# Stick-breaking attention in one hybrid decoder step: Q and K first, then prompt heads and sample pages in one schedule

## The chip, the core and the metric

The kernel runs on one core of one Trainium2 chip. The metric is the device time of one execution in microseconds (us). A core has these engines: PE (TensorE, matrix products and transposes; PEld is its weight load), DVE (VectorE), ACT (ScalarE), POOL (GpSimd) and SP (SyncE, which here issues the DMA transfers). Each executes its own instructions in order and waits on semaphores for the others.

## What is computed

One inference step of a decoder with two layers and model width 1024. Layer 0 mixes tokens by a causal convolution, layer 1 by stick-breaking attention (16 heads of 64); a SwiGLU FFN follows each. There are 512 prompt tokens, and a sample group of 8 sequences with 8 new tokens each, whose 1024 past keys and values lie in a paged pool (8 pages of 128 rows for each sequence, found through a page table). All 576 tokens share the weights. The attention, cut to what matters:

```python
def sb_attend(q, k, v, q_pos, bias):
    z = einsum('bthd,bshd->bhts', q, k) * HEAD_DIM ** -0.5 + bias
    causal = arange(tk) < q_pos
    log_1m_beta = where(causal, -softplus(z), 0.0)
    after = cumsum(log_1m_beta, reverse=True) - log_1m_beta
    a = where(causal, exp(log_sigmoid(z) + after), 0.0)
    return einsum('bhts,bshd->bthd', a, v)
# prompt: q, k, v of the 512 tokens, in blocks of 128 queries
# sample: k and v are the pages of the pool, then the 8 new rows
```

The rows of K and V of all new tokens are outputs too. Everything is fp32.

## The kernel before

Features lie on partitions and tokens in columns (576, as two halves of 288). An fp32 product with weights is made of three products of rounded parts: a tile is split into a high part (`hi`, a cast on ACT) and a low part (`lo`, a subtraction on DVE), and hi·hi, lo·hi and hi·lo are summed. The weights stream in as 512 KB chunks (`wraw`) and are split into `whi` and `wlo`; the activations' parts are `ahi` and `alo`. The attention layer comes in this order:

- The V product (L1372) for all heads. ACT brings each bank to a buffer `vf` (L1378), from which the V rows are stored and the parts `bhi`, `blo` are split.
- Q and K products, 16 chunks of 128 features (`gemm_piece`, L1403), and between them the prompt heads, two per chunk pair `t`. A head's Q and K are split into stacks `qst`, `kst` that hold hi and lo on 128 partitions (L1425 to L1439), so that `z` is two products (L1472) and a causal mask added by a third (L1473). For each block of 128 queries: two sigmoids on ACT, 1-beta (`om`) and beta (`be`) (L1482); the running product of `om`, a scan on DVE (L1492); the weight, a product on POOL (L1499); transposes of the weight on PE (`at`, L1506); the split of the transposed weight into `athi` and `atlo` (L1512 to L1516); and eight products with V (`prompt_o`, L1524). K rows for the output are transposed on PE, copied to the buffer `ktok` (L1457) and stored from SP.
- The order of this stage comes from a list schedule (`graph`, `run_ops`): each operation has an engine, a planned cost and the resources that it reads and writes, and the program emits the operations in planned order. Each engine then keeps that order. A few tables (`LAG`, `Q_AT`, `K_AT`, `K0_AT`, `AT_DVE`) say at which block the next chunk's product goes in and which engine splits.
- The sample's pages: 32 groups (8 sequences, four pairs of pages each), in an order written out by hand (`step(n)`). Each group loads two K pages (`kr`) and two V pages (`vr`) of 512 KB; transposes K on PE (`kt`, L1608, 16 of them), copied to `kts` by ACT and DVE (L1613); makes `sz` for all heads in four blocks of 32 rows (L1628); two sigmoids (L1645, L1651), a scan (L1667) that carries on from the group before, a multiply (L1676); two transposes of the weights (`sat`, L1691) with their copy (L1693); and products with V in four blocks of 32 columns (`so`, L1707).
- The output projection `wo` for the first halves of three of its eight chunks runs at the end of the pages. `ffn(1, ..., 3, ...)` does the rest of it together with the second FFN.

Of the kernel before, what the change touches and what calls it, by code (L numbers as in the profile page):

```python
# [9 lines left out]
F32 = mybir.dt.float32  # L10
# [6 lines left out]
P = 128  # L17
D = 1024
# [23 lines left out]
AT_DVE = (((0, 0, 1, 0), (1, 1, 0, 1)), ((0, 0, 0, 1), (0, 1, 1, 0)), ((1, 0, 1, 1), (0, 0, 1, 0)), ((1, 0, 1, 1), (0, 0, 1, 0)), ((1, 1, 1, 0), (1, 1, 1, 0)), ((0, 1, 1, 0), (0, 0, 0, 1)), ((1, 1, 1, 1), (0, 1, 1, 0)), ((1, 0, 1, 0), (0, 0, 0, 1)))  # L42
LAG = 1
Q_AT = 0
K_AT = 2
K0_AT = (0, 5, 6, 7)
NVR = 8
# [14 lines left out]
def hybrid_step_kernel(  # L62
# [11 lines left out]
    base = ctx.enter_context(tc.tile_pool(name="base", bufs=1))  # L74
# [212 lines left out]
    x = base.tile([P, NT, TOK], F32, name="x")  # L287
    ahi = base.tile([P, NT, TOK], F32R, name="ahi")
    alo = base.tile([P, NT, TOK], F32R, name="alo")
    bhi = base.tile([P, NT, TOK], F32R, name="bhi")  # L290
    blo = base.tile([P, NT, TOK], F32R, name="blo")
    sacc = base.tile([P, TOK], F32, name="sacc")
    rbc = base.tile([P, TOK], F32, name="rbc")
    rtok = base.tile([P, 8], F32, name="rtok")
# [1051 lines left out]
    with tc.tile_pool(name="att", bufs=1) as att:  # L1346
        qkn = [att.tile([P, NT, TS], F32, name=f"{c}n") for c in "qk"]
# [3 lines left out]
        kts = [att.tile([P, NT, GW], F32, name="kts0")]  # L1351
# [5 lines left out]
        with cvps, tc.tile_pool(name="pr", bufs=1) as pp:  # L1357

            for half in range(2):
                cs = slice(half * 512, (half + 1) * 512)  # L1360
                ps = [bank("mm", f"v{half}_{i}") for i in range(4)] + [bank("z", f"v{half}_4")]
                for kp in range(4):
                    whi, wlo, _ = w_next()
                    if half == 0 and kp == 2:
                        stat_a("mix1")
                    if half == 1 and kp == 2:
                        stat_b("mix1")
                    for k2 in range(2):
                        k = 2 * kp + k2
                        for j, (a, w) in enumerate(((ahi, whi), (ahi, wlo), (alo, whi))):  # L1370
                            for i, (c0, n) in enumerate(TT):
                                nc.tensor.matmul(  # L1372
                                    ps[i][0:n, :], a[:, k, c0 : c0 + n], w[:, k2, :],
                                    start=(k == 0 and j == 0), stop=(k == NT - 1 and j == 2),
                                )
                for i, (c0, n) in enumerate(TT):
# [12 lines left out]
            qst = pp.tile([P, 2, 2, TP], F32R, name="qst")  # L1389
            athi = pp.tile([P, 13, P], F32R, name="athi")  # L1390
            atlo = pp.tile([P, 13, P], F32R, name="atlo")
            base = state["got"]
            qfs, kparts, kfs, amat, pos = {}, {}, {}, {}, {}

            gps = {}

            def gemm_piece(t, which, k):
                if k == 0:
                    gps[t, which] = [bank("mm", f"{'qk'[which]}{t}_{i}") for i in range(2)]
                whi, wlo, nk = parts[base + 2 * t + which]  # L1400
                for j, (w, r) in enumerate(((whi, ahi), (whi, alo), (wlo, ahi))):
                    for i in range(2):
                        nc.tensor.matmul(  # L1403
                            gps[t, which][i][:, :HALF], w[:, k, :], r[:, k, HS[i]],
                            start=(k == 0 and j == 0), stop=(k == nk - 1 and j == 2),
                        )

            def gemm_out(t, which):
                parts.pop(base + 2 * t + which)
                f = pp.tile([P, TOK], F32, tag=f"f{which}", name=f"f{which}_{t}", bufs=2 - which)  # L1410
# [181 lines left out]
            def kt(n):  # L1592
                return kts[n % 2]
# [455 lines left out]
```

## Time and profile before

| What | Value |
|---|---|
| time, median of 3 runs | 1605.6 us (1604.29 to 1607.52) |
| the profiled execution, time | 1609.35 us |
| its span, first to last instruction | 1607.6 us |
| mean granted TensorE clock | 0.984 of full speed |
| PE busy | 1510.4 us (94%) |
| PEld busy | 1352.6 us (84%) |
| DVE busy | 1248.0 us (78%) |
| ACT busy | 782.3 us (49%) |
| POOL busy | 407.2 us (25%) |
| DMA, whole span | 180.23 MB, mean 112 GB/s |

A share over the whole span says little here, since the stages have different limits: about 24 of 40 equal slices of the span lie ahead of the pages and show 4 to 103 GB/s (184 in the first); the four slices of the pages show 293 to 407. So the profile is read by stages: a table of busy times by stretch, then single instructions in order of time, whose distances give prices. A busy PE is not PE at its peak, since entries of matmuls overlap in it; the distance from one start to the next is the better price.

### The profile page before, as it was taken

What the parts mean: (1) busy time and instruction counts of PE and PEld (TensorE: products, weight loads), DVE (VectorE), ACT (ScalarE), POOL (GpSimd) and SP (SyncE); (2) the same over time, 40 slices, a digit from 0 to 9 for tenths busy, and PEclk for the clock granted to TensorE, in tenths of its full rate; (3) what the DMA queues carried; (4) which work ended last, traced back from release to release, by engine and by line L of the source; (5) the groups of instructions that cost most, each with busy time, mean ns of one, the idle gap of its engine ahead of it and who ended that gap; (6) DMA issues with size and microseconds to landing.
All of it is one profiled execution on the core that took longest, in us unless ns stands there. A gap on an engine that the chain in (4) does not pass through costs nothing. (4 is left out here: it accounts for less than half of the span.)

```text
span 1607.6 us, 35925 instructions
## 1 busy us (share of the span) xinstructions
PE 1510.4 (94%) x14371; PEld 1352.6 (84%) x14371; DVE 1248.0 (78%) x2155; ACT 782.3 (49%) x1665; POOL 407.2 (25%) x410
## 2 busy tenths in 40 slices
PE   7999989899999999999999988999998999999997
PEld 7996559889999999987988875555797999999997
DVE  5998544699989999982689985555459998999884
ACT  5223123355546545552667664444435554654553
POOL 3110211333323322350244450000132322332210
PEclk9999998999999999999999989999999999999999
DMA  6233001023222233233321227999612222232231
GB/s 184 76 88 87 4 5 38 29 80 92 93 92 89 85 103 93 70 89 95 91 68 43 73 81 293 407 406 398 217 37 66 92 93 94 90 93 93 92 101 64
DMA packets 152047, 180.23 MB, mean 112 GB/s; under 512 B 6106, under 2 KB 130530, under 8 KB 151864
## 3 DMA queue, kind: packets, MB, share of 16 engines
q1 hardware_dynamic: 151448, 176.36, 33.2%
q8 instruction: 113, 1.85, 0.5%
q10 hardware_dynamic: 432, 1.57, 0.3%
q14 instruction: 54, 0.44, 0.1%
HBM read 170.45 MB, written 8.18 MB: 111 GB/s over the span
## 5 line engine op out<-in xcount | busy, mean ns | idle before, releaser
L953 DVE TENSOR_TENSOR wlo<-fs,whi 128x512 fp32r<-128x512 f32 (+1 forms) x256 | 233.5, 913 | 26.8 <-ACT whi L135 18.8
L1095 PE MATMUL fb<-ahi,whi 128*128 128x288 f32 x704 | 210.7, 299 | 14.2 <-ACT ft L135 9.4
L135 ACT CAST whi<-fs 128x512 fp32r<-128x512 f32 (+1 forms) x256 | 157.1, 614 | 134.9 <-PE fb L1095 115.6
L1095 PE MATMUL fb<-xe,whi 128*128 128x288 f32 x1056 | 216.1, 297 | 0.1
L1095 PE MATMUL fb<-alo,whi 128*128 128x288 f32 x704 | 207.7, 295 | 7.9 <-DVE alo L953 7.9
L1095 PE MATMUL fb<-ahi,wlo 128*128 128x288 f32 x704 | 211.1, 300 | 2.3 <-DVE wlo L953 2.3
L1095 PEld LDWEIGHTS fb<-xe,whi 128*128 128x128 f32 x1056 | 170.4, 189 | 0.5 <-issue 0.3
L1095 PE MATMUL fb<-xe,wlo 128*128 128x288 f32 x528 | 159.1, 301 | 2.7 <-DVE wlo L953 2.6
L1095 PEld LDWEIGHTS fb<-ahi,whi 128*128 128x128 f32 x704 | 133.3, 189 | 17.9 <-ACT ft L135 12.4
L1095 PEld LDWEIGHTS fb<-alo,whi 128*128 128x128 f32 x704 | 134.4, 191 | 8.8 <-DVE alo L953 8.8
L1095 PEld LDWEIGHTS fb<-ahi,wlo 128*128 128x128 f32 x704 | 133.2, 189 | 5.0 <-DVE wlo L953 5.0
L953 DVE TENSOR_TENSOR wlo<-wraw,whi 128x512 fp32r<-128x512 f32 (+1 forms) x160 | 124.0, 782 | 5.7 <-ACT whi L135 5.2
L135 ACT CAST whi<-wraw 128x512 fp32r<-128x512 f32 (+1 forms) x160 | 98.0, 613 | 51.8 <-PE fb L1095 46.0
L1095 PEld LDWEIGHTS fb<-xe,wlo 128*128 128x128 f32 x528 | 99.6, 189 | 7.5 <-DVE wlo L953 7.1
L135 POOL TENSOR_TENSOR fs<-wraw 128x512 f32<-128x512 f32 (+1 forms) x32 | 47.1, 1473 | 210.5 <-DVE wlo L953 210.5
L223 ACT CAST whi<-wraw 128x1024 fp32r<-128x1024 f32 (+1 forms) x43 | 44.9, 1044 | 110.7 <-PE cb L585 48.3
L135 POOL TENSOR_TENSOR fs<-wraw,fs 128x512 f32<-128x512 f32 (+1 forms) x64 | 86.0, 1343 | 50.5 <-DVE wlo L953 44.2
L135 POOL TENSOR_TENSOR fs<-fr 128x512 f32<-128x512 f32 (+1 forms) x32 | 43.7, 1364 | 208.3 <-DVE wlo L953 208.3
L1095 PE MATMUL fb<-he,whi 128*128 128x288 f32 x456 | 93.0, 297 | 2.1 <-DVE x L135 2.0
L628 PE MATMUL cb<-up,dg 32*32 32x288 f32 (+1 forms) x3584 | 80.6, 385 | 13.8 <-issue 13.5
L1095 PE MATMUL fb<-bhi,whi 128*128 128x288 f32 x304 | 90.3, 297 | 2.1 <-DVE x L135 2.1
L1095 PE MATMUL fb<-bhi,wlo 128*128 128x288 f32 x304 | 90.1, 296 | 0.0
(375 smaller groups left out, 4078.1 us busy)
## 6 DMA issues: line engine op xcount, KB each, us to landing
kr<-in_cache_k_dram SPq DMA_DIRECT2D x64, 512.0 KB
vr<-in_cache_v_dram SPq DMA_DIRECT2D x64, 512.0 KB
wraw<-in_ffn_w_up_dram SPq DMA_DIRECT2D x44, 512.0 KB
wraw<-in_cv_w_pw_dram SPq DMA_DIRECT2D x24, 512.0 KB
wraw<-in_ffn_w_down_dram SPq DMA_DIRECT2D x24, 512.0 KB
wraw<-in_sb_w_qkv_dram SPq DMA_DIRECT2D x23, 512.0 KB
fr<-in_ffn_w_gate_dram SPq DMA_DIRECT2D x22, 512.0 KB
wraw<-in_ffn_w_gate_dram SPq DMA_DIRECT2D x22, 512.0 KB
```

Source lines behind the costliest of these rows:

```text
L135: ops[i][3](*(a() if callable(a) else a for a in ops[i][4]))
L223: nc.scalar.copy(hi[:, :n], raw[:, :n])
L628: nc.tensor.matmul(banks[bs[i]][rj, 0:n], dgs[d][ri, k, :], ups[t][ri, h * HALF + k : h * HALF + k + n], start=(m == 0), stop=(k >= PET - ...
L953: nc.vector.tensor_sub(dst, a, b.bitcast(F32))
L1095: nc.tensor.matmul(banks[b][:, :HALF], w[:, k, :], r[:, k, :], start=(first and k == 0 and j == 0), stop=(k == nk - 1 and j == 2), skip_gr ...
```

## The change

- V is no longer split. ACT writes it in fp32 to `vt`, which takes the place of `bhi`, and it is stored from there. `blo` becomes room for the transposed weights `at` and the scan outputs `prd`.
- Q and K are kept in fp32 for all tokens (`qf`, `kf`); the 16 chunks of their products come first, with only the transposes of K rows between them. These go out through a tag `sq` of two buffers, which later holds the prompt's `be`.
- Then one list schedule holds eight head pairs and 32 page groups. The pair `t` is emitted ahead of group `3t`. `z` of a pair is two fp32 products of 64 rows each at row positions 0 and 64 (L1439), `prompt_o` fp32 products of 64 columns at column positions 0 and 64 (L1478), so each head of a pair has half of the array's rows, or of its columns. The stacks, the split of the weights and the sum of two output parts go away; the outputs replace Q in `qf` and are split once at the end.
- V pages lie in `ahi` and `alo` (eight places), K pages in `whi` and `wlo` (two groups deep).
- `wo` has two first halves ahead of the FFN; `ffn(1, ..., 2, ...)` does one half more.

The diff, cut to its core:

```diff
-LAG = 1
-Q_AT = 0
-K_AT = 2
-K0_AT = (0, 5, 6, 7)
-NVR = 8
...
+    with cvps, tc.tile_pool(name="att", bufs=1) as att:
+        vflat = flat_of(renew("bhi", "vt", F32))
+        vt = vflat[:, 0 : 4 * D].rearrange("p (i c) -> p i c", c=D)
+        oflat = flat_of(renew("blo", "at", F32))
+        at_ = [oflat[:, e * 13 * P : (e + 1) * 13 * P].rearrange("p (r q) -> p r q", q=P) for e in range(2)]
+        prd = [oflat[:, 26 * P + i * (TP + 4) : 26 * P + i * (TP + 4) + TP + 1] for i in range(2)]
+        qk = [att.tile([P, NT, TOK], F32, name=f"{c}f") for c in "qk"]
+        kts = [att.tile([P, NT, GW], F32, name=f"kts{i}") for i in range(2)]
...
-                    vf = pp.tile([P, 512], F32, tag="vf", name=f"vf{half}_{i}", bufs=2)
-                    nc.scalar.activation(vf[0:n, :], ps[i][0:n, :], AF.Copy, scale=rtok[0:n, i : i + 1])
-                    if i < 4:
-                        hs = slice(4 * half, 4 * half + 4)
-                        vv = vf.rearrange("p (t e c) -> p t e c", e=2, c=DH)
-                        split_to(bhi[:, hs, c0 : c0 + DH], bhi[:, hs, c0 + DH : c0 + P], vv[:, :, 0, :])
-                        split_to(blo[:, hs, c0 + DH : c0 + P], blo[:, hs, c0 : c0 + DH], vv[:, :, 1, :])
-                        nc.sync.dma_start(v_prompt[c0 : c0 + n, cs], vf)
-                    else:
-                        nc.vector.tensor_copy(vn[:, cs], vf[0:n, :])
-                        nc.sync.dma_start(v_sample[:, cs], vf[0:n, :])
...
+            for i, (c0, n) in enumerate(TT):
+                dst = vt[:, i, cs] if i < 4 else vn[:, cs]
+                nc.scalar.activation(dst, ps[i][0:n, :], AF.Copy, scale=rtok[0:n, i : i + 1])
+                nc.sync.dma_start(v_prompt[c0 : c0 + n, cs] if i < 4 else v_sample[:, cs], dst)
...
+        def k_out_put(t, part, b):
+            fs = slice(t * P, (t + 1) * P)
+            ktok = small.tile([P, TOK], F32, tag="sq", name=f"ktok{t}_{part}", bufs=2)
+            if part == 0:
+                nc.scalar.copy(ktok[:, 0:TP], banks[b])
+                nc.sync.dma_start(
+                    k_prompt.rearrange("(i p) f -> p i f", p=P)[:, :, fs],
+                    ktok[:, 0:TP].rearrange("p (i c) -> p i c", c=P),
...
-                for j in range(2):
-                    nc.tensor.matmul(pzt[:, 0:n], qst[:, e, j, qs], kst[:, e, 0:n], start=(j == 0), stop=False)
-                nc.tensor.matmul(pzt[:, qb * P : n], identb, mask, start=False, stop=True)
+        def z_pe(t, qb):
+            n = (qb + 1) * P
+            qs = slice(qb * P, n)
+            for e in range(2):
                 hs = slice(e * DH, (e + 1) * DH)
+                nc.tensor.matmul(
+                    banks[e][:, 0:n], qk[0][hs, t, qs], qk[1][hs, t, 0:n], start=True, stop=False,
+                    tile_position=(e * DH, 0),
                 )
+            for e in range(2):
+                nc.tensor.matmul(banks[e][:, qb * P : n], identb, mask, start=False, stop=True)
...
+        def at_put(e, qb, b, eng):
+            dst = at_[e][:, slice(qb, qb + 3 * qb + 1, 3), :]
+            src = banks[b][:, 0 : (qb + 1) * P].rearrange("p (j q) -> p j q", q=P)
+            (nc.vector.tensor_copy if eng == "D" else nc.scalar.copy)(dst, src)
...
-                for j in range(4):
-                    r = slice(4 * j, 3 * j + 4)
-                    for i, b in enumerate((athi, atlo)):
-                        nc.tensor.matmul(
-                            po[:, j * P : TP], (bhi, blo)[e][:, t, j * P : (j + 1) * P], b[:, r, :],
-                            start=(j == 0 and i == 0), stop=(j == 3 and i == 1),
+        def prompt_o(t, b):
+            for j in range(4):
...
+                    nc.tensor.matmul(
+                        banks[b][hs, j * P : TP], vt[:, j, (2 * t + e) * DH : (2 * t + e + 1) * DH], at_[e][:, r, :],
+                        start=(j == 0), stop=(j == 3), tile_position=(0, e * DH),
+                    )
...
+        def prompt_put(t, b):
+            nc.vector.tensor_copy(qk[0][:, t, 0:TP], banks[b])
...
+                kr = wpool.tile([P, D], F32R, tag=("whi", "wlo")[i], name=f"kr{c}").bitcast(F32)
+                gather(kr, cache_k, c)
+                kraw[n].append(kr)
...
+        def open_v():
+            for tag in ("ahi", "alo"):
+                a = flat_of(renew(tag, f"v_{tag}", F32))
+                vplace.extend(a[:, i * D : (i + 1) * D] for i in range(4))
+                satp.append(a[:, 4 * D : 4 * D + 3 * P].rearrange("p (i c) -> p i c", c=P))
...
-            def do_prep(t):
-                q, k, kst = fq[t], fk[t], ring("kst", 2)
-                bank_of["kst", t] = kst
-                for e in range(2):
-                    do("A", 0.53, [q], [f"qst{e}h"], put_qst, t, e, 0)
-                    do("A", 0.53, [k], [f"{kst}{e}h", "kst"] if e == 0 else [f"{kst}{e}h"], put_kst, t, e, 0)
-                    do("G", 1.23, [q, f"qst{e}h"], [f"qst{e}l"], put_qst, t, e, 1)
-                    if e:
-                        do("G", 1.23, [k, f"{kst}{e}h"], [f"{kst}{e}l"], put_kst, t, e, 1)
-                    else:
-                        do("D", 0.6, [k, f"{kst}{e}h"], [f"{kst}{e}l"], put_kst, t, e, 1)
-                    do("D", 0.33, [f"qst{e}h"], [f"qst{e}x"], put_qst, t, e, 2)
-                    do("D", 0.33, [f"qst{e}l"], [f"qst{e}y"], put_qst, t, e, 3)
-                for i in range(2):
...
+            for qb in (3, 2, 1, 0):
+                f = (qb + 1) / 4
+                do("P", 0.95 * f + 0.1, [f"q{t}", f"k{t}"], ["b0", "b1"], z_pe, t, qb)
...
+                    do("A", 0.14 + 0.43 * f, [f"b{e}"], [f"om{om}"], z_sigmoid, t, e, qb, ombs[om], 0)
+                    do("A", 0.14 + 0.43 * f, [f"b{e}"], [f"be{be}"], z_sigmoid, t, e, qb, bt, 1)
+                    do("D", 0.07 + 0.535 * f, [f"om{om}"], [f"pr{pr}"], z_prod, qb, ombs[om], prd[pr])
+                    do("G", 0.14 + 1.09 * f, [f"be{be}", f"pr{pr}"], [f"om{om}"], z_weight, qb, ombs[om], bt, prd[pr])
...
+            b, name = tr()
+            do("P", 1.2, [f"at{e}_{qb}" for e in range(2) for qb in range(4)] + ["vt"], [name], prompt_o, t, b)
+            do("D", 0.55, [name], [f"q{t}"], prompt_put, t, b)
...
+                    do("P", 0.43, [w + "hl"[i]], [name], k_pe, n, i, hf, bk)
+                    do("AD"[hf], 0.5, [name], [kn[-1]], k_put, n, i, hf, bk)
...
+            do("P", 1.05, [*kn, f"qbd{b % 2}"], ["b2"], s_z, n)
+            do("A", 0.33, ["b2"], [so], s_sig, n, 0)
+            do("D", 0.4, [so, f"sc{(n - 1) % 2}"], [sc], s_scan, n)
+            do("A", 0.33, ["b2"], [be], s_sig, n, 1)
+            do("D", 0.37, [be, sc], [so, f"ax{b % 2}"] if g == 3 else [so], s_mul, n)
...
-            for g in range(len(steps) + LAG):
-                t, i = divmod(g, 8)
-                if i == 0 and t < NT:
-                    do_prep(t)
-                if t + 1 < NT and i == Q_AT:
-                    do_gemm(t + 1, 0)
-                if t + 1 < NT and i == K_AT:
-                    do_gemm(t + 1, 1)
...
+        do("A", 0, [], ["be0", "be1"], open_be)
+        do("Q", 0, [], ["a", *[f"v{i}" for i in range(8)], "sat0", "sat1"], open_v)
+        do("A", 0, [], ["rbc", "sbe0", "sbe1"], nothing)
+        for n in range(NG):
+            if n % 3 == 0 and n // 3 < NT:
+                do_prompt(n // 3)
+            if n == 3 * NT:
+                do("A", 0, [], ["bb", "vt", *[f"at{e}_{qb}" for e in range(2) for qb in range(4)], "pr0", "pr1"], open_b)
+                for t in range(NT):
+                    do("A", 0.55, [f"q{t}", "bb"], [f"bh{t}"], out_split, 0, t, slice(0, TP))
+                    do("D", 0.67, [f"q{t}", f"bh{t}"], [f"bl{t}"], out_split, 1, t, slice(0, TP))
+            if n >= NG - 3:
+                do("Q", 2.9, [], [ring("raw", RAWS), "ld"], wo_load)
+            do_group(n)
...
-        ffn(1, n_before_wo, 3, 0, n_before_fin)
+        ffn(1, n_before_wo, 2, 0, n_before_fin)
```

Three places show how it moves instructions. First PE, in the middle of the prompt heads. Before (`z` and `at` are the heads, `k` the K product of the next pair):

```order
L1472 MATMUL z_1_9767<-kst_9583,qst 128x256 x2
L1473 LDWEIGHTS identb
L1473 MATMUL z_1_9767<-mask,identb 128x128
L1506 MATMUL at_3_9771<-ident,om_3_9713 128x128 x4
L1403 MATMUL k_0_9718<-ahi,whi_9554 128x288
L1403 MATMUL k_1_9719<-ahi,whi_9554 128x288
L1403 MATMUL k_0_9718<-alo,whi_9554 128x288
L1403 MATMUL k_1_9719<-alo,whi_9554 128x288
L1403 MATMUL k_0_9718<-ahi,wlo_9555 128x288
L1403 MATMUL k_1_9719<-ahi,wlo_9555 128x288
L1506 MATMUL at_2_9790<-ident,om_2_9743 128x128 x3
L1472 MATMUL z_0_9795<-kst_9583,qst 128x128 x2
```

After (`ab` are banks, `kf,qf` is `z` of a pair, `at,vt` is `prompt_o`, `kr` a K page):

```order
L1439 MATMUL ab_8541<-kf,qf 128x512
L1439 MATMUL ab_8542<-kf,qf 128x512
L1444 LDWEIGHTS identb
L1444 MATMUL ab_8541<-mask,identb 128x128
L1444 LDWEIGHTS identb
L1444 MATMUL ab_8542<-mask,identb 128x128
L1478 MATMUL ab_8545<-at,vt 64x512 x2
L1478 MATMUL ab_8545<-at,vt 64x384 x2
L1478 MATMUL ab_8545<-at,vt 64x256 x2
L1478 MATMUL ab_8545<-at,vt 64x128 x2
L1529 MATMUL ab_8548<-ident,kr_9874 128x128 x4
L1529 MATMUL ab_8545<-ident,kr_9874 128x128 x4
```

Between the pieces of a head stood K products, whose inputs were long there; now page transposes stand there, and head products in pairs.

Second ACT. Before, in the first chunk pairs (`qst`, `kst` and `athi` are casts for the parts, `of` is one half of an output):

```order
L1435 CAST qst<-f_1_8878 64x512
L1416 COPY qn<-f_1_8878 128x64
L1516 CAST athi<-at_0_8895 128x128
L1482 ACTIVATE om_3_8911<-z_3_8897,bias_bc 128x512
L1482 ACTIVATE be_3_8915<-z_3_8897,bias_bc 128x512
L1482 ACTIVATE om_2_8933<-z_2_8917,bias_bc 128x384
L1482 ACTIVATE be_2_8938<-z_2_8917,bias_bc 128x384
L223 CAST whi_8940<-wraw_8889 128x1024
L1425 CAST kst_8963<-f_1_8921 64x512
L1539 COPY of_8973<-po_8924 64x512
L1482 ACTIVATE om_1_8981<-z_1_8969,bias_bc 128x256
L1482 ACTIVATE be_1_8983<-z_1_8969,bias_bc 128x256
```

After, where the products end and the heads begin (`ktok` are K rows for the output):

```order
L1424 COPY ktok_0_9435<-ab_8547 128x512
L1430 COPY ktok_1_9450<-ab_8546 64x128
L1424 COPY ktok_0_9482<-ab_8545 128x512
L1430 COPY ktok_1_9485<-ab_8548 64x128
L1424 COPY ktok_0_9517<-ab_8547 128x512
L1430 COPY ktok_1_9548<-ab_8546 64x128
L1448 ACT_TABLE_LOAD
L1448 ACTIVATE omb_8206<-ab_8541,bias_bc 128x512
L1448 ACTIVATE omb_8207<-ab_8542,bias_bc 128x512
L1430 COPY ktok_1_9559<-ab_8548 64x128
L1448 ACTIVATE be_9564<-ab_8541,bias_bc 128x512
L1448 ACTIVATE be_9565<-ab_8542,bias_bc 128x512
```

The casts between the sigmoids are gone; the copies of K rows, two for each chunk pair, now stand in one row ahead of the first sigmoid.

Third SP, which issues the transfers. Before, in the first two chunk pairs:

```order
L1458 DMA out_dram<-ktok_8789 128x4x128
L1462 DMA out_dram<-ktok_8789 64x128
L204 DMA wraw_8889<-in_sb_w_qkv_dram 128x8x128
L204 DMA wraw_8966<-in_sb_w_qkv_dram 128x8x128
L1458 DMA out_dram<-ktok_9055 128x4x128
L1462 DMA out_dram<-ktok_9055 64x128
L204 DMA wraw_9096<-in_sb_w_qkv_dram 128x8x128
L204 DMA wraw_9263<-in_sb_w_qkv_dram 128x8x128
```

After, at the end of the products:

```order
L1425 DMA out_dram<-ktok_0_9435 128x4x128
L1431 DMA out_dram<-ktok_1_9450 64x128
L1425 DMA out_dram<-ktok_0_9482 128x4x128
L1431 DMA out_dram<-ktok_1_9485 64x128
L1425 DMA out_dram<-ktok_0_9517 128x4x128
L1499 TENSOR_LOAD pgt
L1499 ISA x2
L1501 ISA
L1501 DMA kr_9520<-in_cache_k_dram 128x1024
```

The stores of K rows stood between loads of weights; now they follow each other, and the first K page (`kr`) stands behind the last large one.

## Rows read from the trace of the kernel before

**Rows 1.** Windows; columns: stretch, its length, busy time (entries) by engine, clock, DMA.
```profile
768.00:968.00 200.00, 185.07 (x1292) 168.24 (x1291) 173.60 (x339) 133.99 (x274) 92.70 (x93) 0.96 0.23 69
968.00:1152.00 184.00, 171.01 (x1769) 100.34 (x1766) 95.55 (x211) 84.81 (x196) 5.58 (x21) 1.00 0.95 364
1000.00:1120.00 120.00, 115.03 (x1220) 64.68 (x1221) 64.21 (x143) 54.76 (x132) 3.76 (x15) 1.00 1.02 404
1240.00:1280.00 40.00, 38.70 (x286) 37.84 (x285) 39.32 (x65) 24.65 (x53) 12.59 (x11) 1.00 0.30 93
```

**Rows 2.** Timeline of PE; start, duration, line, out<-in, shape, entries [idle before <-releaser].
```profile
768.18 0.40 PE L1403 MATMUL q<-ahi,whi 128*128 128x288 f32 x1
...
775.13 0.43 PE L1403 MATMUL k<-ahi,whi 128*128 128x288 f32 x2
...
781.53 0.43 PE L1403 MATMUL q<-ahi,whi 128*128 128x288 f32 x2
...
1152.29 0.37 PE L320 MATMUL fb<-bhi,whi 128*128 128x288 f32 x1 [1.81 <-DVE fb L135]
```

**Rows 3.** Timeline of PE among the sample's pages.
```profile
974.59 1.97 PE L1608 MATMUL kt<-ident,kr 128*128 128x128 f32 x16
976.48 1.47 PE L1628 MATMUL sz<-kts,qbd 128*32 128x256 f32 x16
...
986.12 0.66 PE L1608 MATMUL kt<-ident,kr 128*128 128x128 f32 x4
986.71 1.07 PE L1628 MATMUL sz<-kts,qbd 128*32 128x256 f32 x16
987.71 0.66 PE L1608 MATMUL kt<-ident,kr 128*128 128x128 f32 x4
988.30 0.64 PE L1707 MATMUL so<-vr,satr 128*32 128x256 f32 x8
988.87 0.66 PE L1608 MATMUL kt<-ident,kr 128*128 128x128 f32 x4
...
991.27 1.10 PE L1628 MATMUL sz<-kts,qbd 128*32 128x264 f32 x16
```

**Rows 4.** Groups by line, 768 to 968; busy us, mean ns | idle before.
```profile
L1492 DVE TENSOR_TENSOR_SCAN pr<-om,zer 128x512 f32<-128x512 f32 (+1 forms) x64 | 62.8, 984 | 8.2 <-ACT om L1482 7.7
...
L1482 ACT ACTIVATE om<-z,bias_bc 128x512 f32<-128x512 f32 (+1 forms) x64 | 33.8, 529 | 31.0 <-PE z L1473 30.8
...
L1512 DVE TENSOR_TENSOR atlo<-at,athi 128x512 fp32r<-128x512 f32 (+3 forms) x61 | 28.7, 484 | 3.6 <-ACT athi L1516 2.6
...
L1514 DVE CAST athi<-at 128x256 fp32r<-128x256 f32 (+3 forms) x32 | 15.2, 479 | 3.0 <-PE at L1506 1.9 <-PE po L1524 0.5
...
L1516 ACT CAST athi<-at 128x512 fp32r<-128x512 f32 (+3 forms) x30 | 13.1, 438 | 12.5 <-PE at L1506 11.8 <-PE po L1524 0.4
```

**Rows 5.** Groups by line among the pages, 972 to 1132.
```profile
L1613 DVE COPY kts<-kt 128x512 f32<-128x512 f32 x61 | 42.2, 692 | 41.4 <-PE kt L1608 41.1
...
L1613 ACT COPY kts<-kt 128x512 f32<-128x512 f32 x62 | 36.4, 587 | 76.2 <-PE kt L1608 75.4 <-DVE blo L1547 0.9
L1667 DVE TENSOR_TENSOR_SCAN sp<-so,sp,zer 128x256 f32<-128x256 f32 x22 | 16.4, 745 | 0.0
L1645 ACT ACTIVATE so<-sz,bias_hq 128x256 f32<-128x256 f32 (+1 forms) x30 | 14.6, 488 | 0.1
...
L1676 DVE TENSOR_TENSOR so<-rbc,sp 128x256 f32<-128x256 f32 x30 | 12.8, 426 | 3.1
```

**Rows 6.** The page's costliest groups: the convolution's taps in the array's blocks.
```profile
L628 PE MATMUL cb<-up,dg 32*32 32x288 f32 (+1 forms) x3584 | 80.6, 385 | 13.8 <-issue 13.5
```

**Rows 7.** Timeline of ACT at V's evictions (`vf` is stored and has two buffers).
```profile
736.44 1.27 ACT L1378 ACTIVATE vf<-v,rtok 128x512 f32<-128x512 f32 x2 [5.05 <-PE v L1372]
...
742.13 0.69 ACT L1378 ACTIVATE vf<-v,rtok 128x512 f32<-128x512 f32 x1 [1.68 <-DMA out_dram<-vf]
```

More of the change, by code (lines that the diff above doesn't have):

```diff
@@ new lines, in gemm_out, with k_out_pe @@
+        def gemm_out(t, which, bs):
+            parts.pop(c_qk + 2 * t + which)
+            for i, b in enumerate(bs):
+                nc.vector.tensor_mul(qk[which][:, t, HS[i]], banks[b][:, :HALF], rbc[:, HS[i]])
+        def k_out_pe(t, part, b):
+            for i in range(4) if part == 0 else (4,):
+                c0, n = TT[i]
+                nc.tensor.transpose(banks[b][0:n, i % 4 * P : (i % 4 + 1) * P], qk[1][:, t, c0 : c0 + n], ident)
+        def k_out_put(t, part, b):
[6 more added lines that the diff above has]
+                    ktok[:, 0:TP].rearrange("p (i c) -> p i c", c=P),
+                )
+            else:
+                nc.scalar.copy(ktok[0:TS, 0:P], banks[b][0:TS, 0:P])
+                nc.sync.dma_start(k_sample[:, fs], ktok[0:TS, 0:P])
@@ new lines, in gather, with load_k @@
+        def gather(dst, src, c):
+            with tc.issue_after(issued[-4]) if len(issued) >= 4 else nullcontext():
+                r = nc.sync.value_load(pgt[0:1, c : c + 1], min_val=0, max_val=src.shape[0] - 1)
+            page = src[bass.ds(r, 1)]
+            issued.append(nc.sync.dma_start(dst, page.rearrange("g p d -> (g p) d")).ins)
+        def load_k(n):
+            b, g = groups[n]
+            kraw[n] = []
+            for i in range(2):
+                c = b * NPG + 2 * g + i
+                kr = wpool.tile([P, D], F32R, tag=("whi", "wlo")[i], name=f"kr{c}").bitcast(F32)
+                gather(kr, cache_k, c)
+                kraw[n].append(kr)
@@ new lines, in k_pe, with k_put, width @@
+        def k_pe(n, i, hf, bk):
+            for j in range(4):
+                t = 4 * hf + j
+                nc.tensor.transpose(banks[bk][:, j * P : (j + 1) * P], kraw[n][i][:, t * P : (t + 1) * P], ident)
+        def k_put(n, i, hf, bk):
+            dst = kts[n % 2][:, 4 * hf : 4 * hf + 4, i * P : (i + 1) * P]
+            (nc.scalar.copy, nc.vector.tensor_copy)[hf](dst, banks[bk].rearrange("p (j c) -> p j c", c=P))
+        def width(n):
+            return GW if groups[n][1] == 3 else 2 * PAGE
@@ new lines, in s_z @@
+        def s_z(n):
+            b, g = groups[n]
+            w, pz, q, k = width(n), banks[2], qbd[b % 2], kts[n % 2]
+            for t in (0, 2, 4, 6, 1, 3, 5, 7):
+                r = 32 * (t // 2)
+                nc.tensor.matmul(
+                    pz[r : r + 32, 0:w], q[:, t, :], k[:, t, 0:w], start=(t % 2 == 0),
+                    stop=(t % 2 == 1 and g != 3), tile_position=(0, r),
+                )
+            if g == 3:
+                nc.tensor.matmul(
+                    pz[:, 2 * PAGE : GW], repq.rearrange("p h q -> p (h q)"), mask[0:NQ, 0:NQ], start=False, stop=True
+                )
@@ new lines, in s_at_put, with s_o @@
+        def s_at_put(n, bk):
+            at = satp[n % 2]
+            nc.scalar.copy(at[:, 0:2, :], banks[bk][:, 0 : 2 * P].rearrange("p (i c) -> p i c", c=P))
+            if groups[n][1] == 3:
+                nc.vector.tensor_copy(at[0:TS, 2, :], banks[bk][0:TS, 2 * P : 3 * P])
+        def s_o(n, i, s):
+            g = groups[n][1]
+            a, v = (satp[n % 2][:, i], vplace[s]) if i < 2 else (satp[n % 2][0:TS, 2], vn)
+            for c in range(4):
+                r = slice(32 * c, 32 * c + 32)
+                nc.tensor.matmul(
+                    banks[3][r, 0:256], a[:, r], v[:, c * 256 : (c + 1) * 256],
+                    start=(g == 3 and i == 0), stop=(g == 0 and i == 1), tile_position=(0, 32 * c),
+                )
@@ new lines, in open_b, with out_split, wo_mm @@
+        def open_b():
+            nonlocal_b.extend((renew("bhi", "bhi1", F32R), renew("blo", "blo1", F32R)))
+        nonlocal_b = []
+        def out_split(part, ts, cs):
+            hi, lo = nonlocal_b
+            src = qk[0][:, ts, cs]
+            if part == 0:
+                nc.scalar.copy(hi[:, ts, cs], src)
+            else:
+                nc.vector.tensor_sub(lo[:, ts, cs], src, hi[:, ts, cs].bitcast(F32))
+        def wo_mm(t, b):
+            mm_half(parts[wo_c + t], *nonlocal_b, 0, banks[b])
```

714 lines of the change are left out of this document (228 added, 486 removed).

## The prediction

> **What bounds the kernel now.** I read the windows first, as a table by stage, then single TensorE instructions in time order, then groups by line. [rows 1] shows the two stages that the change joins. In 768–968 us (Q and K products with the prompt heads between them) TensorE (PE) is busy for 185.07 of 200 us, VectorE (DVE) for 173.60, ScalarE (ACT) for 133.99, and the DMA engines for 0.23 of the time. In 968–1152 us (the sample's pages) PE is busy for 171.01 of 184, DVE for only 95.55, and the DMA engines for 0.95 at 364 GB/s. In its middle, 1000–1120, the DMA share is 1.02 at 404 GB/s: pages set the pace there, engines wait for them. So one stage is short of engines with idle DMA, the other the reverse; joining them is worth something only as far as PE has room, because PE is nearly full in both.
>
> The first Q product starts at 768.18 and the second FFN's first product at 1152.29 [rows 2]. All that the change touches lies in these **384.1 us**, but for V's evictions (left at nothing: they lie under V's own products). The sum below is the same stretch after, made against the profiled execution's own time, 1609.35 us (span 1607.6, the rest lies around it); it is 3.7 us above the median of 1605.6, and a difference carries over from one to the other.
>
> **The change part by part.**
>
> *Prices on PE.* One Q or K chunk (48 products of 288 columns) takes from 775.13 to 781.53, 6.40 us [rows 2]. Sixteen transposes of a page stand 1.89 us apart from the next kind of work, four 0.59 [rows 3]: 0.108 each, 0.84 ns per column, and some 0.16 for the change of kind. The eight z matmuls of a group in four row blocks take 1.00, its o matmuls in four column blocks 0.57 [rows 3]; less the change of shape they are 0.86 and 0.43. These are 1024 and 512 columns for each block, at 0.84 ns: four blocks run side by side at the price of one, and a fp32 product makes two passes (8 matmuls, 16 entries). From the same rows a pair of changes (into a blocked shape and out) costs about 0.30.
>
> *Products.* 16 × 6.40 = 102.4; transposes of K rows, 40 × 0.108 = 4.3. Nothing lies between them any more.
>
> *Pages.* A group is 1.73 + 0.86 + 0.86 + 0.22 (two transposes) = 3.67, and with its three pairs of changes 4.57. The trace has groups 4.56 apart where nothing is late (986.71 to 991.27, [rows 3]), so the prices close. 24 groups: 88.1, with new-token work 4.5 and 45 changes at 0.30 (the listing has 60 four-column blocks for 32 groups) 13.5: 106.1. Eight groups: 35.4.
>
> *Heads.* Removed on other engines: the casts and subtractions that made hi/lo stacks, with 28.7 us of DVE in the low parts of the weights alone [rows 4]. On PE a head pair's z is 1280 columns in two passes, 1280 × 1.68 ns = 2.15; its o the same; together 34.4 for eight pairs if the two heads of a pair run side by side. No row of before shows two 64-row or 64-column blocks. The nearest rows: four blocks at the full four-fold price [rows 3], and the conv taps, 32×32 blocks, where 3584 entries of 288 columns took 80.6 [rows 6]; one after another at 0.84 ns per column they would be 867, so sixteen blocks gave 10.8, 0.67 of sixteen. I take side by side (nearer in kind: few blocks, one direction); by 0.67 z and o would come to 51 (+17), and with no overlap to 69 (+34). Weight transposes 160 × 0.108 = 17.3. Masks: 64 of 128 columns, between nothing and a transpose each; half, 3.5. About 40 changes of shape, 0 to 0.30 each; 12. Heads: 67.2.
>
> The Trainium skill (TensorE: Matmul & The Clock Gate, Measured speedup vs the span model) gives 3.07-fold for four row blocks where [rows 3] bear out close to four. By its share z and o would be 45 and not 34, and the sum 12 longer.
>
> *How full PE gets.* 24 groups and all head pairs are emitted together (pair t before group 3t): 173.3 us of PE work. DVE there: scans 62.8, its half of the weight copies 32 × 0.479 = 15.3 [rows 4], page copies 48 × 0.692 = 33.2, page scans 24 × 0.745 = 17.9, page multiplies 24 × 0.426 = 10.2 [rows 5], small ones 16: 155. ACT: sigmoids 2 × 33.8, weight copies 32 × 0.438 = 14.0 [rows 4], page copies 48 × 0.587 = 28.2, page sigmoids 48 × 0.488 = 23.4 [rows 5], small ones 13: 146. All three engines are in chains through each other and follow one fixed order. The same kind of order brought the fullest engine to 173.60 of 200 where it was DVE and to 0.925 where it is PE [rows 1], the latter counting engine time that my prices hold. I take 0.87: 199 us; then DVE is at 0.78. The last eight groups stand alone, 35.4 at 0.96 (1000–1120, [rows 1]): 37. The 32 groups load 2.1 MB each (four pages of 512 KB), 67 MB; at 404 GB/s 166 us of the 236, so the pages are hidden; if DVE or PE took under 166, DMA would bound again.
>
> *The junction.* In before K rows left between weights over the whole stretch. Now their transposes crowd into the last 3.7 of 16 chunks, and from the third on every large copy of them uses one buffer and waits for the store before to land. A store of the same size landed 4.4 us after its copy (copies end 737.71, the next starts at 742.13 on the DMA, [rows 7]), with other transfers beside it. Six such waits of 3 to 5 us with the copy stand against 18 us of products left. Queued behind on ACT are the first sigmoids, on SP the first K pages; PE has only one z pair to do meanwhile. Price 0 to 14, and even at 0 the first pair has a chain to fill; I take 6.
>
> *End.* A wo half is 24 products, half a chunk, 3.2; two remain, one moves into the FFN, where it costs the same: 9.6. Draining the last group: 4.
>
> Sum: 102.4 + 4.3 + 199 + 37 + 6 + 4 + 9.6 = 362.3 against 384.1, a gain of 21.8. Predicted: 1609.35 − 21.8 = 1587.6 for a profiled execution, and **1584** for the median. PE's bare work hardly shrinks; what goes is idle time at pages and at hi/lo preparation.
>
> **The rivals.**
>
> *Full packing.* The order fills PE as the FFN does, 38.70 of 40 in 1240–1280 [rows 1], pages being a large stock of independent work, and the junction hides. 208.7 / 0.97 = 215: 102.4 + 4.3 + 215 + 2 + 9.6 = 333, gain 51, **1555**. Against it: page transposes wait for banks that DVE and ACT empty, so the filler depends on the engines it should fill for.
>
> *DVE sets the heads' pace (the other side).* The planner counts a prompt scan at 0.20 to 0.60, 0.40 on average; the trace has 0.984 [rows 4]. Page copies are counted at 0.5 and take 0.692 [rows 5]. So the fixed order puts PE's transposes earlier than their inputs exist, on every head, and PE, in order, holds the pages behind them. For it: PE waited in before too, and there product pieces, which wait for nothing on DVE, stood between. Against it: DVE has 155 us in 199. It decides from 221 us for that stage (2.7 more for each head pair), PE at 0.78; at 0.76 it takes 228, 29 more: **1613**.
>
> *Pairs don't run side by side.* 34.4 / 0.87 = 40 more: **1624**. If they gain only the conv taps' share, 17 / 0.87 = 20 more: **1604**, no change. For it: no row shows such a pair. Against: [rows 3].
>
> *PE has far more room than its busy share says.* Weight loads fill only 100.34 of 184 us in the pages' stage [rows 1]. If that were the true load, heads would vanish under the pages' 166 us: 102.4 + 4.3 + 166 + 6 + 4 + 9.6 = 292, **1514**. The priced group of 4.57 against 4.56 measured speaks against it: PE has no hole there. The Trainium skill (Perfetto Trace Analysis, Identifying the Most-Contended Engine) says to judge TensorE by weight-load time and not by matmul busy time; here the price per column disagrees, since 32-column loads are short and their products long.
>
> **How the numbers follow.** Forecast, 1584 within some 16 either way, 0.50; full packing 0.17; DVE's pace 0.13; no overlap 0.09; the taps' share 0.08; room by loads 0.03. The range holds 8 in 10: it leaves out no overlap, the loads' case and the lower part of full packing, and ends at DVE's price: 1553 to 1614. A measurement tells 0.2%, 3.2 us, from no change. Faster: forecast, packing, loads and a little of the taps' case, 0.71. Same: most of the taps' case and edges of others, 0.10. Slower: 0.19.
>
> **What would show it.** Q/K chunks 6.4 apart without gaps. A 512-column z pair (L1439), two entries for each head, 0.86 to its mask; 1.7 if serial; the same for o (L1478). Between the last product and the first s_z (L1543) under 10 us; else the junction is the miss, with ACT's K-row copies waiting for DMA. From the first z pair to the last prompt_o some 200 us, with DVE at 0.78 and PE at 0.87; at 220 and PE waiting for POOL's weights or DVE's copies it is DVE's pace. DMA under 0.8 there. A granted clock under 0.96 in 870–1070 would say that the mixed work lowered it, which I don't count.

## The result

| | before | after |
|---|---|---|
| time, median | 1606.56 us (4 runs, 1604.29 to 1608.45) | 1655.82 us (4 runs, 1651.70 to 1657.99) |
| ratio, 95% interval | | 1.0304 (1.0279 to 1.0329) |
| span of the profiled execution | 1607.6 us | 1654.3 us |
| mean granted TensorE clock | 0.984 | 0.975 |

The changed kernel is 3% slower; a gain of 1.4% was forecast. The windows of the changed kernel, in the columns of [rows 1]:

```profile
768.84:876.50 107.66, 107.44 (x809) 106.72 (x808) 31.27 (x47) 23.16 (x32) 0.24 (x1) 1.00 0.30 90
876.50:905.20 28.70, 19.78 (x101) 11.00 (x100) 13.75 (x29) 15.19 (x31) 8.68 (x13) 0.76 0.50 173
905.20:1108.80 203.60, 175.80 (x1517) 97.24 (x1516) 117.87 (x264) 109.58 (x255) 53.69 (x71) 0.95 0.63 218
1108.80:1189.00 80.20, 62.30 (x616) 38.73 (x610) 36.71 (x73) 33.50 (x72) 0.70 (x3) 0.96 0.75 263
```

The products take 107.7 us. From the first z pair (876.5) to the first page product (905.2) the clock is 0.76, and PE is idle for 8.9 of the 28.7 us. The stage with heads and pages lasts until 1108.8, with no engine full: PE 175.80 of 203.60, part of it at a low clock, DVE 117.87, DMA 0.63. Then eleven groups of pages stand alone; they and two `wo` halves last until the FFN starts at 1191.5. That stretch is no fuller: PE 62.30 of 80.20, DVE under half, DMA 0.75, where before had a share of 1.02. The FFN behind takes 462.8 us (455.3 before).

No engine is scarce there, so the suspect was the order, that is, steps that wait for each other. The pages alone show it best. PE of the changed kernel, one group of pages after the heads (L1543 is `sz`, L1529 the K transposes, L1587 the transposes of the weights, L1603 the products with V):

```profile
1144.64 1.09 PE L1543 MATMUL ab<-kts,qbd 128*32 128x256 f32 x16
1145.66 0.66 PE L1529 MATMUL ab<-ident,kr 128*128 128x128 f32 x4
1148.12 0.63 PE L1529 MATMUL ab<-ident,kr 128*128 128x128 f32 x4 [1.80 <-DMA kr<-in_cache_k_dram]
1148.59 0.38 PE L1587 MATMUL ab<-ident,somb 128*128 128x128 f32 x2
1149.75 0.66 PE L1529 MATMUL ab<-ident,kr 128*128 128x128 f32 x4 [0.79 <-ACT v_ahi L1593]
1150.34 1.07 PE L1603 MATMUL ab<-v_alo,v_ahi 128*32 128x256 f32 x16
1151.22 1.09 PE L1543 MATMUL ab<-kts,qbd 128*32 128x256 f32 x16
```

From one group's z (L1543) to the next are 6.6 us, some of it a wait for a K page; over nine groups, from 1110.88 to 1173.10, 6.9, against the 4.56 of [rows 3]. The row that tells why is 1149.75: a transpose of K pages waits for ACT's copy `v_ahi` (L1593), which is the copy of the transposed *weights* of the group at hand (they lie behind the V pages in `ahi` and `alo`). Nothing in the arithmetic asks for that. The listing of PE a group earlier shows the bank:

```text
L1543 MATMUL ab_8543<-kts_8189,qbd_8193 32x256 x8
L1529 MATMUL ab_8547<-ident,kr_12586 128x128 x4
L1603 MATMUL ab_8544<-v_ahi 32x256 x4
L1529 MATMUL ab_8546<-ident,kr_12668 128x128 x4
L1587 MATMUL ab_8548<-ident,somb_8198 128x128 x2
L1529 MATMUL ab_8547<-ident,kr_12668 128x128 x4
L1529 MATMUL ab_8548<-ident,kr_12586 128x128 x4
```

Four banks are handed out in turn, in the order in which the list is written: four K transposes of a group, then its weights. In the changed kernel (cut from `tr` and `do_group`):

```python
        def tr():
            b = 4 + slot("tr", 4)
            return b, f"b{b}"
...
            for i in range(2):
                for hf in range(2):
                    bk, name = tr()
                    do("P", 0.43, [w + "hl"[i]], [name], k_pe, n, i, hf, bk)
...
            bk, name = tr()
            do("P", 0.25, [so] + [f"ax{b % 2}"] * (g == 3), [name], s_at_pe, n, bk)
```

The weights of one group and the last K transpose of the next (both `ab_8548` here) follow each other in one bank. So that K transpose waits for the weights' copy, and the next group's z waits for it: z, sigmoid, scan, multiply, transpose, copy, K transpose, copy, z, one group after another. The direct waits of K transposes for the weights' copies are only 4.2 of the 80.2 us (for ACT 2.5, for DVE 1.7); PE's other waits lie mostly at other steps of this chain, 5.3 us of them at the multiply. So the trace makes the chain likely, and the runs have to show it.

### The profile page after: what moved, and what is told of

It is laid out like the page before. It is cut to its first block, busy times and chain, and to the rows that moved or that the text cites. A ratio compares the mean times of both kernels' runs of the same rounds, so it can differ in the third digit from the quotient of the medians.

```text
span 1654.3 us, 35491 instructions
## 1 busy us (share of the span) xinstructions
PE 1527.6 (92%) x14371; PEld 1345.1 (81%) x14371; DVE 1175.8 (71%) x2011; ACT 745.9 (45%) x1585; POOL 373.0 (23%) x386
## 5 line engine op out<-in xcount | busy, mean ns | idle before, releaser
L228 DVE TENSOR_TENSOR wlo<-wraw,whi 128x1024 fp32r<-128x1024 f32 (+1 forms) x44 | 55.8, 1267 | 59.0 <-ACT whi L217 57.3
L1529 PE MATMUL ab<-ident,kr 128*128 128x128 f32 x512 | 80.8, 291 | 16.3 <-ACT kts L1533 3.1
```

The source lines that it names most:

```text
L228: nc.vector.tensor_sub(lo, raw, hi.bitcast(F32))
L1529: nc.tensor.transpose(banks[bk][:, j * P : (j + 1) * P], kraw[n][i][:, t * P : (t + 1) * P], ident)
```

## The experiments

Two theories on the main loss: the **banks' turn** (above), and the **wrong costs** of the plan, by which PE meets steps whose inputs are not there (the mechanism of the rival on DVE's pace). Beside them the **junction** as a loss of its own. Before itself measured 1606.56 us beside the result, 1609.03 beside e1 to e4, 1605.96 beside e5 to e8 and 1609.88 beside e9 to e11; so differences of medians between these sets are good to some 4 us, and the ratios to before are the better measure.

**K rows spread over the products** (e1_junction). In `k_out_put` and in the list of the products:

```diff
-            ktok = small.tile([P, TOK], F32, tag="sq", name=f"ktok{t}_{part}", bufs=2)
+            ktok = flat_of(kts[t % 2])[:, t // 2 * 512 : t // 2 * 512 + 512]
...
+                ktok = oflat[0:TS, 13 * P + t * P : 14 * P + t * P]
...
+                    after = [f"ko{t - 1}0", f"ko{t - 1}1"] if t and which and k == 0 else []
```

> The changed kernel, but the K rows for the output are planned between the chunk pairs of the products (pair t's K product waits in the plan for the rows of pair t-1) and go through eight places of their own in kts and at, so that no store has to land before another copy and the prompt's beta buffers are free. If the junction is the main loss (products end at 876.5 us, PE waits 7.6 us for the beta sigmoid, the clock is at 0.67 to 0.87 until 918, the first s_z comes at 905): 20 us or more are gained, 1635 or less. If the pages' order is the main loss, only the idle time and part of the low clock come back: 1641 to 1650, with the page groups after the heads still some 6.5 us apart.

Measured: 1641.12 us (ratio to before 1.0197, 1.0164 to 1.0230), 14.7 under the changed kernel. The junction is a loss, not the main one: the groups behind the heads are still 7.5 us apart. In the changed kernel it reads so (ACT, then PE):

```profile
872.83 0.59 ACT L1424 COPY ktok<-ab 128x512 f32<-128x512 f32 x1 [3.38 <-PE ab L1418]
...
876.57 0.59 ACT L1424 COPY ktok<-ab 128x512 f32<-128x512 f32 x1 [3.00 <-PE ab L1418]
...
878.62 1.27 ACT L1448 ACTIVATE omb<-ab,bias_bc 128x512 f32<-128x512 f32 x2
879.78 0.25 ACT L1430 COPY ktok<-ab 64x128 f32<-64x128 f32 x1
885.01 1.27 ACT L1448 ACTIVATE be<-ab,bias_bc 128x512 f32<-128x512 f32 x2 [4.98 <-DMA out_dram<-ktok]
```

```profile
876.53 1.43 PE L1439 MATMUL ab<-kf,qf 64*128 64x512 f32 x4
877.89 0.28 PE L1444 MATMUL ab<-mask,identb 128*128 128x128 bf16 x2
885.75 2.22 PE L1439 MATMUL ab<-kf,qf 64*128 64x384 f32 x4 [7.57 <-ACT be L1448]
```

The large copies kept pace with the products after all: two of them had waited 2.4 and 2.3 us for a store, but the last two wait for PE alone. What was late is `be`: its buffer holds the last small K rows, whose store stands on SP behind the first K pages and lands at 885. From the last product to the first page product, in the changed kernel and then in e1:

```profile
876.05:905.18 29.13, 20.21 (x103) 11.26 (x100) 14.18 (x30) 15.19 (x31) 8.68 (x13) 0.77 0.49 171
876.40:890.49 14.09, 13.43 (x90) 8.32 (x87) 10.43 (x25) 9.84 (x24) 6.09 (x8) 1.00 0.82 261
```

The stretch is 15.0 us shorter: idle time of PE falls from 8.9 to 0.7 us, and the clock is 1.00 and not 0.77.

**Banks parted between heads and pages**, two and two (e2_rings): `tr(4, 2)` in the heads, `tr(6, 2)` in the groups.

> The changed kernel, but the four banks in which transposes land are parted: two for the heads, two for the pages. If heads and pages hold each other up because all take these banks in one fixed turn (the heads' stage of 232 us then shrinks): 1635 to 1645. The page groups after the heads would not be helped by it, since with two banks the last K transposes of a group still wait for the weights of the group before (6.5 to 7.5 us apart as now). If the shared turn does not matter, two banks for each are only fewer: 1656 to 1670.

Measured: 1649.58 us (1.0252, 1.0218 to 1.0286), 6 under the changed kernel, between the two expectations. The stage from the first page product to the last head shrinks from 203.6 to 177.7 us:

```profile
886.40:1064.10 177.70, 161.94 (x1382) 90.35 (x1382) 119.62 (x264) 106.77 (x255) 63.66 (x77) 0.95 0.65 223
```

But it holds 17 groups and not 21. By PE's entries it runs at 7.8 a us, against 7.5 in the changed kernel and 9.0 in the next run, so the heads are little freer. 15 groups are left to run alone, 8.0 us apart, slower than with the common turn. Heads and pages together take 300 us where the changed kernel has 286; what is gained lies at the junction, 13.3 us from the first z pair to the first page product for 28.7. So that heads and pages hold each other up is at most a small part of the loss.

**K transposes a group ahead** (e3_pipe). The list is written in another order; banks and costs stay:

```diff
+            held[n] = kn, vs
+
+        def do_rest(n):
+            b, g = groups[n]
+            kn, vs = held.pop(n)
             so, sc, be = f"so{n % 3}", f"sc{n % 2}", f"sbe{n % 2}"
...
             do_group(n)
+            if n:
+                do_rest(n - 1)
+        do_rest(NG - 1)
```

> The changed kernel, but in the list the K transposes of group n+1 come ahead of the rest (z, sigmoids, scan, weights, output) of group n; costs and banks stay. Theory of the banks' turn: five banks are taken in turn for each group, four for K and one for the weights, so that the last K transposes of a group wait in the plan and on the chip for the weights of the group before, and the groups run one after another (6.9 us apart after the heads, against 5.2 that the DMA allows). Then this order frees them: 5.2 to 5.5 apart after the heads, 1625 to 1640. Theory of the wrong costs: the plan still puts PE's steps too early, groups stay over 6.2 apart, 1650 or more.

Measured: **1601.10** us (0.9951, 0.9935 to 0.9968), 55 under the changed kernel and below before. That is more than the theory of the banks' turn had forecast, since the stage with heads gained too:

```profile
875.30:905.00 29.70, 21.49 (x105) 12.64 (x104) 14.01 (x29) 15.75 (x33) 9.77 (x14) 0.71 0.51 174
905.00:1069.60 164.60, 154.96 (x1480) 91.62 (x1478) 116.37 (x262) 104.78 (x252) 57.42 (x70) 0.99 0.76 267
1069.60:1138.00 68.40, 60.26 (x650) 39.15 (x645) 37.11 (x76) 36.49 (x78) 0.71 (x3) 1.00 0.84 313
```

PE is busy for 0.94 of the stage with heads, at a clock of 0.99, with the same heads and 21 groups (1480 entries for 1517) in 164.6 us instead of 203.6. Behind the heads z of the groups follow 5.0 us apart (ten starts from 1073.03 to 1118.20), and what PE waits for most there is the DMA:

```profile
1111.23 1.33 PE L1543 MATMUL ab<-kts,qbd 128*32 128x256 f32 x14
...
1115.57 1.09 PE L1529 MATMUL ab<-ident,kr 128*128 128x128 f32 x8 [1.23 <-DMA kr<-in_cache_k_dram]
1116.83 1.09 PE L1529 MATMUL ab<-ident,kr 128*128 128x128 f32 x8 [0.16 <-DMA kr<-in_cache_k_dram]
1117.76 0.38 PE L1587 MATMUL ab<-ident,somb 128*128 128x128 f32 x2
1118.20 1.34 PE L1543 MATMUL ab<-kts,qbd 128*32 128x256 f32 x14
```

In this list the last K transpose of a group still shares its bank with weights, but with those of two groups before.

**Costs of the trace in the plan** (e4_costs): a page scan 0.9 for 0.4, a prompt scan 0.2 + 1.05f for 0.07 + 0.535f, and so on.

> The changed kernel, but the planned costs of scans, weight products, page copies, page sigmoids and weight copies are the durations of the trace (a 512-column scan 1.25 and not 0.60, a page scan 0.9 and not 0.4, page sigmoids 0.48 and not 0.33, page copies 0.59 and 0.69 and not 0.5). Theory of the wrong costs: PE's waits for scans and multiplies (11 us in the groups by pages alone, more among the heads) go, 1635 or less. Theory of the banks' turn: the order hardly changes what waits for what, 1648 to 1660, groups after the heads over 6 us apart.

Measured: 1651.07 us (1.0256, 1.0225 to 1.0286), 5 under the changed kernel, with groups still 6.9 apart: the wrong costs are not what made it slow.

**A bank of its own for the page weights** (e5_satbank). The reordering changes the place in the list and the turn at once; this changes the bank alone:

```diff
-            b = 4 + slot("tr", 4)
+            b = 4 + slot("tr", 3)
...
-            bk, name = tr()
+            bk, name = 7, "b7"
```

> The changed kernel with its own order of the list, but the page weights' transposes (and the output's) take a bank of their own, the eighth, and K transposes and heads take turns on the other three. Theory of the banks' turn: what made the groups run one after another was a K transpose that takes the bank of the former group's weights, so most of what the reordering gave back (54 us) comes back without any reordering: 1600 to 1620, groups after the heads under 6 us apart. If instead the gain came from the place in the list (which step the plan takes first), a bank of its own changes little and three banks for the rest cost something: 1650 to 1665.

Measured: **1600.02** us (0.9955, 0.9939 to 0.9972). Behind the heads eight distances of z, from 1056.30 to 1093.58, are 4.7 us on average, and no K transpose waits for weights there:

```profile
1089.29 1.07 PE L1543 MATMUL ab<-kts,qbd 128*32 128x256 f32 x16
1090.18 0.62 PE L1603 MATMUL ab<-v_alo,v_ahi 128*32 128x256 f32 x8
1090.72 1.99 PE L1529 MATMUL ab<-ident,kr 128*128 128x128 f32 x16
1092.64 0.64 PE L1603 MATMUL ab<-v_alo,v_ahi 128*32 128x256 f32 x8
1093.21 0.44 PE L1587 MATMUL ab<-ident,somb 128*128 128x128 f32 x2
1093.58 1.10 PE L1543 MATMUL ab<-kts,qbd 128*32 128x264 f32 x16
```

Two edits that have in common only that K transposes no longer follow the former group's weights in a bank give the same time. With that the cause is shown.

**Together.** The reordered list with the K rows spread (e6_pipe_junction), with the heads spread as well (e7_spread_heads), and with the costs of the trace (e8_pipe_junction_costs):

> The reordered list (K transposes of group n+1 ahead of the rest of group n) together with the K rows spread over the products and stored from places of their own. If the two losses are separate, their gains of 55 and 15 us add up: 1584 to 1589. If the pages are by then bound by the DMA, the earlier start of the heads is waited away behind them: 1593 to 1600.

> As the run before, and the head pairs are put ahead of groups 0, 4, 8, 12, 15, 19, 22, 26 and not of every third, so that the last ten groups don't stand alone; the splits of the outputs come before group 30. With the reordered list the stage with heads has PE busy for 0.94 and DMA for 0.76, and the rest has DMA at 0.84 with PE waiting for K pages. If the two only lay unevenly, both stages together shrink by about 10 to 15 us: 1570 to 1577. If the outputs' splits and the first halves of the output projection, which now have only two groups to hide behind, come late, it is the same or up to 10 longer than the run before.

> The reordered list with the K rows spread, and the planned costs of the trace. If wrong costs are a loss of their own (5 us alone), it is 3 to 8 us under the run with the old costs; if the steps have slack once the groups overlap, it is within 3 us of it.

Measured: 1590.00 (0.9893, 0.9871 to 0.9915), 1590.32 (0.9894, 0.9864 to 0.9924) and 1579.91 us (0.9836, 0.9811 to 0.9862). The first lies between its two expectations: the junction's gain is smaller beside the reordering, 11 for 14.7 us, or 0.6 for 1.1% by the ratios, though their intervals overlap. Spreading the heads, for which 10 to 15 or nothing were expected, gave nothing here: the last head ends 26 us later (1085.4 for 1059.0) and the rest is 25 us shorter. The costs are worth 10 us beside the reordering, more than either expectation. That is 0.6%, where they are worth 0.5% alone; with these intervals the two are not told apart, and why the costs help stays open. Windows of e8:

```profile
870.60:892.00 21.40, 20.99 (x140) 14.31 (x139) 14.06 (x29) 14.03 (x31) 10.12 (x11) 1.00 0.71 240
892.00:1047.20 155.20, 151.26 (x1479) 89.98 (x1477) 114.05 (x261) 105.07 (x253) 55.48 (x71) 1.00 0.76 282
1047.20:1117.50 70.30, 60.41 (x650) 39.97 (x646) 37.64 (x77) 35.41 (x77) 1.15 (x3) 0.98 0.82 307
```

PE is at 0.98 in the junction and 0.97 with heads, as full as the FFN in [rows 1].

The same with the bank of its own for the reordering (e9), with both (e11), and with the bank and spread heads (e10):

> The changed kernel's own order of the list, with a bank of its own for the page weights, the K rows spread over the products and the planned costs of the trace. The bank alone gave the same 1600 as the reordering, so with the other two it should come to the same 1578 to 1583 as the reordered list with them. If the reordering does something that the bank does not, it stays at 1588 or more.

> The reordering and the bank of its own at once, with the K rows spread and the planned costs of the trace. If both cure the same wait, the second adds nothing: 1577 to 1583. If three banks for K and heads are then too few, 1584 or more.

> As the run with a bank of its own, K rows spread and costs of the trace, and the head pairs put over 28 groups. With the reordered list and old costs that spread gave nothing (1590.3 against 1590.0): what the pages after the heads lost was gained by heads that came later. The same is expected here, 1577 to 1584; if the costs are what kept it from paying, 1565 to 1575.

Measured: 1581.94 (0.9831, 0.9806 to 0.9856), 1582.08 (0.9828, 0.9803 to 0.9852) and **1576.40** us (0.9805, 0.9781 to 0.9828). Bank and reordering cure the same wait and don't add up. The last is the best version found, 2% under before, just below its first expectation; whether the spread itself gives its 5.5 us is not certain, since its interval and that of e9 overlap.

## Why the prediction was wrong

The forecast and the trace of the changed kernel, by the terms of the sum (us):

| term | forecast | measured |
|---|---|---|
| products and K-row transposes | 106.7 | 107.7 |
| first z pair to last head, with the junction | 205, with 24 groups | 232.3, with 21 |
| pages alone, drain, two wo halves | 47.4, for 8 groups | 82.7, for 11 |
| FFN behind, more than before | 3.2 | 7.5 |

**Prices held.** z of a pair at 512 columns takes 1.06 and its eight o products 2.30, changes included:

```profile
929.17 1.13 PE L1439 MATMUL ab<-kf,qf 64*128 64x512 f32 x4
930.23 0.28 PE L1444 MATMUL ab<-mask,identb 128*128 128x128 bf16 x2
930.45 2.37 PE L1478 MATMUL ab<-at,vt 128*64 128x512 f32 x16
932.75 0.66 PE L1529 MATMUL ab<-ident,kr 128*128 128x128 f32 x4
```

The sum had 0.86 and 2.15, with 0 to 0.30 for a change: the halves run side by side, and the rivals on pairs fall. The Trainium skill (TensorE: Matmul & The Clock Gate, Measured speedup vs the span model) has 3.07 of 4 for four row blocks; for two no share like that is lost here.

**The step that failed is "how full PE gets".** I took 0.87 for the stage with heads, from a stage of the kernel before whose list had other resources, and 0.96 for pages alone, from a hand-written order that has four groups under way. Neither carries over to a list whose groups share four banks in one turn. By my prices the heads' stage with the junction holds 67.2 + 21 × 4.42 = 160 us of PE work, 0.69 of 232.3, where the forecast had 173.3 in 205, or 0.85; the pages alone hold 11 × 4.42 + 6.4 = 55, 0.67 of 82.7. What took the place of that packing is the wait of each group for the weights of the one before. I counted work and occupancy, and never followed one group from z to the next z through the names in the list: `tr()` is called once for each K transpose and once for the weights. Five calls on a ring of four is all that had to be seen.

The busy share would have misled even afterwards. PE is busy for 175.80 of 203.60 us, 0.86, which looks like the 0.87 that I forecast. It is a coincidence: with the banks free (e3) the same heads and groups take 154.96 us of busy PE. Of the 39 us between the two stages 18 are idle time of PE (27.8 against 9.6), and 21 are nearly the same work taking longer, at a clock of 0.95 for 0.99.

The term for pages alone had a second fault. I took 37 us for eight groups from PE's share, although my own DMA figure, 2.1 MB for a group at 404 GB/s, makes 5.2 us a group and 41.5 for eight. In e3 the groups are 5.0 apart, with PE waiting for K pages.

The Trainium skill (Perfetto Trace Analysis, Optimization Strategy) says that the same gap repeating on the engine that should be saturated can mean that SBUF or PSUM has no room for the next tile. The gap at each group is of this kind, and the remedy was not more room: with the same eight banks e3 and e5 lose it.

**The rival on DVE's pace** had the side right and the mechanism wrong: correcting the costs in the plan gave 5 us (e4), where the banks gave 55. My remark under full packing, that page transposes wait for banks, named the resource and stopped there.

**The junction** was priced at 6. The longest idle stretch of PE was 7.57, and removing it gave 14.7. The step that failed there is that I priced the wait and not the clock with it: 876.5 to 905.2 passes at 0.76, the same stretch of e1 at 1.00. The wait was also another than the six stores I named.

**The clock** I left out, but for the sign of under 0.96. In the table of windows it is 0.95 over the heads and 0.96 over the pages alone; in e3 it is 0.99 and 1.00 there, in e5 1.00 and 0.92. So it is not the mix of heads and pages that lowers it; how much of the loss is the clock and how much the waits was not parted.

**The FFN** took 7.5 us more and not 3.2. The other 4.3 were not followed up; the clock is 0.66 from 1189 to 1199.

**What the estimate was good for.** With banks and junction mended (e6) the way from the first product to the FFN takes 361.0 us, where the sum had 359.1 without the moved half. The junction and heads take 187 us with 21 groups and the rest 69 with eleven; with three groups at 5.0 moved across, 202 and 54, against 205 and 47. So part of the agreement is two misses of opposite sign. The forecast of 1584 was that of a kernel in which no group waits for the former one's bank.

## What to carry to other kernels

When a list schedule hands out buffers in turn, the order in which the list is written is part of the schedule: follow one unit of work through the ring, and count the calls per unit against its length, before trusting any share of busy time. Where no engine of a stage is full, look in the trace for a wait whose releaser has no arithmetic link to the waiter; here it named the shared buffer. A stall of PE can cost more than its length: here 8.2 us less idle time made the stretch 15.0 us shorter, as the clock did not fall.

## What was not expected of the hardware

From the products to the FFN the granted clock of the changed kernel is at 1.00 or at 0.50 (2.4 or 1.2 GHz), and the values between in the tables are averages of the two. Three stretches behind the junction:

```profile
881.50:891.70 10.20, 5.95 (x20) 3.68 (x20) 2.73 (x6) 3.74 (x7) 2.94 (x3) 0.50 0.88 297
898.50:912.20 13.70, 10.81 (x86) 6.54 (x84) 10.30 (x20) 8.26 (x17) 5.61 (x5) 1.00 0.55 190
912.20:919.00 6.80, 6.80 (x46) 3.28 (x44) 1.55 (x4) 2.29 (x6) 0.00 (x0) 0.50 0.60 200
```

```profile
908.03 0.66 PE L1529 MATMUL ab<-ident,kr 128*128 128x128 f32 x4 [0.62 <-ACT kts L1533]
910.95 0.44 PE L1587 MATMUL ab<-ident,somb 128*128 128x128 f32 x2 [2.27 <-DVE somb L1578]
...
912.30 1.11 PE L1529 MATMUL ab<-ident,kr 128*128 128x128 f32 x4
913.35 1.08 PE L1603 MATMUL ab<-v_ahi 128*32 128x256 f32 x8
```

It fell to 0.50 at 881.5, within the 7.57 us in which PE had nothing to do, rose at 891.7, fell once more for 3.4 us, and was back at 1.00 from 898.5. It fell again at 912.2, after idle gaps of 0.62 and 2.27 us, and then four K transposes take 1.05 us (912.30 to 913.35) where [rows 3] have 0.59, although PE is busy for all of these 6.80 us. In e8, where PE is busy for 20.99 of 21.40 us at the junction, the clock stays at 1.00. So the same matmuls ran at either level, and work that came after a gap paid for it.
